# Attention's value products traced one half of the queries later, with the edge key blocks at 128 queries

## The chip, the cores and the metric

The kernel runs on one core of a Trainium2 chip. Its time is what the device takes for one execution of the whole program, in microseconds (us). The engines are named as the profile names them: PE is TensorE (with PEld, its weight loader), DVE is VectorE, ACT is ScalarE, POOL is GpSimd, SP is SyncE, whose queue starts most of the loads.

## What is computed

One layer of a hybrid encoder over 2048 tokens of width 1024, all in float32: a norm, one projection, banded attention beside an RWKV-7 recurrence, a gated merge, and a feed-forward part. The change touches the attention alone:

```python
# 8 heads of 64; a chunk is 64 tokens; a query sees its own chunk and the 8 before
scores = einsum('bnqhd,bnkhd->bnhqk', qc, kb) * 64 ** -0.5
scores = where(valid, scores + bias, -1e30)     # learned bias on clipped distance
p = softmax(scores, axis=-1)
out = einsum('bnhqk,bnkhd->bnqhd', p, vb)       # the value products
```

## The kernel before

**Float32 in two parts.** TensorE multiplies numbers rounded to its own float32r type. To keep float32 accuracy, an operand is split into a high part (ScalarE's rounding copy) and a low part (VectorE: source less high part), and a product is made of several matmuls. `split` (L65 to L67) does it for dense operands, `mm3` (L69 to L77) multiplies high by high, high by low and low by high.

**Stages.** The tokens go in four groups of 512. For each group there is a stage of the recurrence, then `phase_attention` (L915), then `phase_merge`. The feed-forward part follows after all four.

**Attention.** A group's 8 heads are four pairs (`att_pair`, L787). A pair first has its queries, keys and values projected (`dense`, L106; 24 matmuls of 512 columns each). The pools hold two pairs' `QA`, `QB`, `KK` and `VV`, so a pair can be projected while the one before it is in its softmax. Then, for each head of the pair (`par`) and each half of the group's queries (`half`, 256 queries), two blocks (`b`) of 128 queries go through:

1. scores against 640 keys into a PSUM tile that has one buffer (L851);
2. bias added and minimum taken by VectorE (L857), exponential by ScalarE (L862), scaling by VectorE (L865);
3. five transposes of 128 by 128 by TensorE (L869), again with one buffer;
4. the high part of the transposed probabilities, `PTh`, by ScalarE (L873), and the low part, `PTl`, by VectorE (L874).

A half's 256 queries see six key blocks of 128 (`kt` 0 to 5): the first block of queries sees 0 to 4, the second 1 to 5. So `PTh` and `PTl` are tiles of 128 x 6 x 256 in which two corners hold zeros, written once a group (L932, L933). There are two such pairs of tiles, used in turn. The value products of a half (L875 to L886) are twelve matmuls of 256 columns into one PSUM tile: the six key blocks with `PTh`, then the six with `PTl`. The stationary operand holds the values' high and low parts side by side, so the result's lower 64 rows and upper 64 rows are added afterwards: a copy (L883) and an addition into `ya` (L884). In the first group there are no keys before the group, so a half has two key blocks (4 and 5) or four (2 to 5). After a pair's four halves `ya` is split (L887) for the projection that follows.

**Other work at hand.** The second branch's projection (`branches`, L954, with the weights of `proj_b`) is traced at the end of `phase_attention`; its inputs come from the recurrence and don't wait for the attention.

**What sets the order.** The program is traced in Python and ordered by a planner when it is built. The planner follows each engine with estimated durations and gives it, among the instructions whose inputs and buffers it believes ready, the one that was traced first. Semaphores then keep the data right on the chip; an engine takes its instructions in the planned order and waits where an input is late. The order of tracing is thus an order of precedence, not the order of execution: with the tracing of before, a half's value products stand ahead of the next half's scores, and all of a pair's work ahead of the next pair's projections.

Of the kernel before, what the change touches and what calls it, by code (L numbers as in the profile page):

```python
# [2 lines left out]

# [5 lines left out]
F32 = mybir.dt.float32  # L9
# [3 lines left out]
ALU = mybir.AluOpType  # L13
# [36 lines left out]
class Block:  # L50
# [736 lines left out]
    def att_pair(self, g, p):  # L787
        nc, ap = self.nc, self.ap
        rows = [slice(0, C), slice(C, P)]
        first, lastg = g == 0, g == self.NG - 1  # L790
        KK = ap.tile([P, 2, 2, G], F32R, tag="KK", name="KK")
        VV = ap.tile([P, 2, GT, 2, 2, C], F32R, tag="VV", name="VV")
        if not first:
            kr = ap.tile([P, 2, G], F32, tag="kr", bufs=1, name="kr")
            nc.sync.dma_start(kr, self.kc[p])
            nc.scalar.copy(KK[:, :, 0], kr)
            vr = ap.tile([P, GT, 2, 2, C], F32, tag="kr", bufs=1, name="vr")
            nc.sync.dma_start(vr, self.vc[p])
            nc.scalar.copy(VV[:, 0], vr)

        ps = self.dense(ATT0 + p * P)
        QA = ap.tile([P, 2, G], F32R, tag="QA", name="QA")
        QB = ap.tile([P, 2, G], F32R, tag="QB", name="QB")
        for par in range(2):
            rw, ow = rows[par], rows[1 - par]
            nc.scalar.activation(QA[rw, par], ps[rw], AF.Copy, scale=-0.125)
            nc.scalar.activation(QB[ow, par], ps[rw], AF.Copy, scale=-0.125)
            for dst in (QB[rw, par], QA[ow, par]):
                nc.vector.scalar_tensor_tensor(
                    dst, ps[rw], -0.125, QA[rw, par].bitcast(F32), op0=ALU.mult, op1=ALU.subtract  # L810
                )
        ps = self.dense(ATT0 + HW + p * P)
        for par in range(2):
            rw, ow = rows[par], rows[1 - par]
            nc.scalar.copy(KK[rw, par, 1], ps[rw])
            nc.vector.tensor_tensor(KK[ow, par, 1], ps[rw], KK[rw, par, 1].bitcast(F32), ALU.subtract)
        ps = self.dense(ATT0 + 2 * HW + p * P)
        vf = ap.tile([P, G], F32, tag="vf", bufs=1, name="vf")
        nc.scalar.copy(vf, ps)
        pst = self.pt.tile([P, GT, P], F32, tag="t", name="ps_vt")  # L820
        for t in range(GT):
            nc.tensor.transpose(pst[:, t], vf[:, t * P : (t + 1) * P], self.ident)
        pv4 = pst.rearrange("p t (e d) -> p t e d", d=C)
        for t in range(GT):
            nc.scalar.copy(VV[:, 1, t, :, 0], pv4[:, t])
            nc.vector.tensor_tensor(VV[:, 1, t, :, 1], pv4[:, t], VV[:, 1, t, :, 0].bitcast(F32), ALU.subtract)
        if not lastg:
            nc.gpsimd.dma_start(self.kc[p], KK[:, :, 1].bitcast(F32))
            nc.gpsimd.dma_start(self.vc[p], VV[:, 1].bitcast(F32))

        ya = ap.tile([P, G], F32, tag="ya", name="ya")
        for par in range(2):
            bias = self.load_bias(2 * p + par)
            Kv = KK[:, par].rearrange("p h n -> p (h n)")
            for half in range(2):
                PTh, PTl = self.pts[self.npt % 2]
                self.npt += 1
                for b in range(2):
                    qb = half * 2 + b
                    k0 = qb * P if not first else G  # L840
                    n = (qb + 5) * P - k0
                    s0 = 640 - n
                    h1 = (n // 2) if n > 512 else n
                    pss = self.psc.tile([P, 1024], F32, tag="s", name="ps_s")
                    c0 = 512 - h1 if n > 512 else 0
                    qs = slice(qb * P, (qb + 1) * P)
                    for lo_, w in ((0, h1), (h1, n - h1)):
                        if not w:
                            continue
                        for i, q in enumerate((QA, QB)):  # L850
                            nc.tensor.matmul(  # L851
                                pss[:, c0 + lo_ : c0 + lo_ + w], q[:, par, qs],
                                Kv[:, k0 + lo_ : k0 + lo_ + w], start=i == 0, stop=i == 1,
                            )
                    sc = ap.tile([P, 640], F32, tag="sc", name="sc")
                    mn = ap.tile([P, 1], F32, tag="mn", bufs=4, name="mn")
                    nc.vector.tensor_tensor_reduce(  # L857
                        sc[:, 0:n], bias[:, s0:640], pss[:, c0 : c0 + n], 1.0, 3.0e38,
                        ALU.add, ALU.min, mn,
                    )  # L860
                    sm = ap.tile([P, 1], F32, tag="sm", bufs=4, name="sm")
                    nc.scalar.activation(sc[:, 0:n], sc[:, 0:n], AF.Exp, scale=-1.0, bias=mn, accum_out=sm)  # L862
                    rs = ap.tile([P, 1], F32, tag="rs", bufs=4, name="rs")
                    nc.vector.reciprocal(rs, sm)
                    nc.vector.tensor_scalar(sc[:, 0:n], sc[:, 0:n], rs, None, ALU.mult)  # L865
                    nk = n // P
                    pst = self.pt.tile([P, 5, P], F32, tag="t", name="ps_pt")
                    for j in range(nk):
                        nc.tensor.transpose(pst[:, j], sc[:, j * P : (j + 1) * P], self.ident)  # L869
                    kt0 = b + 5 - nk  # L870
                    hv = PTh[:, kt0 : kt0 + nk, b * P : (b + 1) * P]
                    lv = PTl[:, kt0 : kt0 + nk, b * P : (b + 1) * P]
                    nc.scalar.copy(hv, pst[:, 0:nk])  # L873
                    nc.vector.tensor_tensor(lv, pst[:, 0:nk], hv.bitcast(F32), ALU.subtract)  # L874
                pv = self.pv.tile([P, 2 * P], F32, tag="pv", name="ps_pv")  # L875
                kts = [kt for kt in range(6) if not first or half * 2 + kt >= GT]
                terms = [(x, kt) for x in (PTh, PTl) for kt in kts]
                for i, (x, kt) in enumerate(terms):
                    kb = half * 2 + kt
                    st = VV[:, kb // GT, kb % GT, par].rearrange("p s d -> p (s d)")  # L880
                    nc.tensor.matmul(pv, st, x[:, kt], start=i == 0, stop=i == len(terms) - 1)
                y2 = ap.tile([C, 2 * P], F32, tag="y2", name="y2")
                nc.scalar.copy(y2, pv[C:P])  # L883
                nc.vector.tensor_tensor(  # L884
                    ya[rows[par], half * 2 * P : (half + 1) * 2 * P], pv[0:C], y2, ALU.add
                )  # L886
        self.split(self.ya[0][:, p], self.ya[1][:, p], ya)  # L887

    def build_bias(self, sp, dp):

# [24 lines left out]
    def phase_attention(self, g):  # L915
        tc, nc = self.tc, self.nc
        self.yctx = ExitStack()
        yp = self.yctx.enter_context(tc.tile_pool(name="ya", bufs=1, side="right", reuse_waits="tile"))
        self.ya = self.alloc_y(yp)
        self.bp = self.yctx.enter_context(tc.tile_pool(name="br", bufs=2, side="right", reuse_waits="tile"))  # L920
        with ExitStack() as ctx:
            e = ctx.enter_context
            self.ap = e(tc.tile_pool(name="at", bufs=2, reuse_waits="tile"))
            pp = e(tc.tile_pool(name="atp", bufs=1, reuse_waits="tile"))
            self.psc = e(tc.tile_pool(name="atps", bufs=1, space=PSUM, reuse_waits="tile"))
            self.pt = e(tc.tile_pool(name="atpt", bufs=1, space=PSUM, reuse_waits="tile"))
            self.pv = e(tc.tile_pool(name="atpv", bufs=2, space=PSUM, reuse_waits="tile"))
            self.pts, self.npt = [], 0
            for i in range(2):
                t = [pp.tile([P, 6, 2 * P], F32R, name=f"PT{x}{i}") for x in "hl"]  # L930
                for y in t:
                    nc.gpsimd.memset(y[:, 0, P : 2 * P].bitcast(F32), 0.0)  # L932
                    nc.gpsimd.memset(y[:, 5, 0:P].bitcast(F32), 0.0)  # L933
                self.pts.append(t)
            for p in range(NP):
                self.att_pair(g, p)
            y = self.load_y(pp, self.ap)
            for i in range(KB // 2):
                nc.gpsimd.dma_start(self.md[i], self.branches(y, 1, i))
# [411 lines left out]
```

## Time and profile before

| | |
|---|---|
| median of 3 runs | 3420.65 us (3418.1 to 3421.2) |
| profiled execution | 3419.56 us, span of its instructions 3417.9 us |
| granted TensorE clock, mean | 0.988 |
| busy: PE, PEld, DVE, ACT, POOL | 96%, 78%, 71%, 41%, 12% |
| value products, L881 | 672 matmuls, in four stages between 340.3 and 1990.8 us |
| scores, L851 | 448 matmuls |
| transposes of probabilities, L869 | 560 |

A row of the profile gives line, engine, operation, the tiles written and read, the shape and the count, then busy time and the mean duration of one. In the timeline the first two columns are the start and the length in us, and brackets hold the idle time of that engine just before, with what ended it. A matmul's bar includes the time that its results take to come out, so bars overlap and the distance between starts tells more than a bar's length. A weight load (PEld) comes ahead of each matmul and may run while the matmul before it is still busy.

### The profile page before, as it was taken

Reading aid. Unit: us, or ns where it says so; the run is one execution under the profiler, and the core shown is the slowest. Engines: PE = TensorE matmul, PEld = TensorE weight load, DVE = VectorE, ACT = ScalarE, POOL = GpSimd, SP = SyncE. Lnnn points to the kernel's source line nnn. Section 1 sums busy time; section 2 is a strip of 40 time slices with the busy share of each in tenths; the row PEclk is TensorE's granted clock in tenths of the full one; section 3 lists DMA queues with packets and bytes.
Section 4 is the critical chain, followed back from the end, with each engine's and each line's share of the span. In section 5 each row is a group of like instructions: output and inputs, shape, how many; then the busy total and the mean of one; then the engine's idle time right before and its main releaser. Section 6 shows DMA issues by size and latency. Waiting matters only on the chain. (4 is left out here: it accounts for less than half of the span.)

```text
span 3417.9 us, 50375 instructions
## 1 busy us (share of the span) xinstructions
PE 3297.4 (96%) x19233; PEld 2675.8 (78%) x19233; DVE 2413.0 (71%) x4110; ACT 1414.0 (41%) x2319; POOL 419.8 (12%) x796
## 2 busy tenths in 40 slices
PE   7999999999999999999999989999999999999998
PEld 5777777777877777877777878888888878888886
DVE  5774856766866665875775875877887788676667
ACT  4434634436644445644445634333321243331112
POOL 2110002111022110021210000111200011100001
PEclk9999999999999999999999999999999999999999
DMA  5224353125373225374224276434845364343333
GB/s 147 84 81 129 131 188 120 56 88 188 122 276 115 62 93 168 124 270 127 74 92 140 91 271 215 136 114 156 290 161 178 105 234 136 114 145 99 99 99 111
DMA packets 397864, 481.10 MB, mean 141 GB/s; under 512 B 17516, under 2 KB 304432, under 8 KB 397624
## 3 DMA queue, kind: packets, MB, share of 16 engines
q1 hardware_dynamic: 346168, 364.63, 33.6%
q0 software_dynamic: 23040, 79.71, 6.1%
q10 hardware_dynamic: 28416, 33.56, 2.9%
q8 instruction: 151, 2.47, 0.3%
q14 instruction: 89, 0.73, 0.1%
HBM read 356.16 MB, written 124.81 MB: 141 GB/s over the span
## 5 line engine op out<-in xcount | busy, mean ns | idle before, releaser
L75 PE MATMUL ps_dn<-fop 128*128 128x512 f32 x3072 | 700.8, 390 | 2.0 <-DVE u L1229 2.0
L75 PEld LDWEIGHTS ps_dn<-fop 128*128 128x128 f32 x3072 | 575.6, 188 | 123.5 <-DVE u L1229 3.5
L75 PE MATMUL psd<-hh,whi 128*128 128x512 f32 x1344 | 543.2, 404 | 7.5 <-ACT whi L66 6.6
L75 PE MATMUL psd<-hl,whi 128*128 128x512 f32 x1344 | 542.5, 404 | 0.0
L75 PE MATMUL psd<-hh,wlo 128*128 128x512 f32 x1344 | 538.9, 401 | 0.6 <-DVE wlo L67 0.5
L66 ACT CAST whi<-wraw 128x1024 fp32r<-128x1024 f32 x232 | 243.3, 1049 | 511.0 <-PE psd L75 410.2
L1229 DVE TENSOR_TENSOR u<-u,ps_dn 128x512 f32<-128x512 f32 x480 | 323.2, 686 | 149.2 <-PE ps_dn L75 148.3
L67 DVE TENSOR_TENSOR wlo<-wraw,whi 128x1024 fp32r<-128x1024 f32 x232 | 282.9, 1220 | 203.0 <-ACT whi L66 185.1
L75 PEld LDWEIGHTS psd<-hh,whi 128*128 128x128 f32 x1344 | 257.4, 192 | 60.6 <-ACT whi L66 7.4
L75 PEld LDWEIGHTS psd<-hh,wlo 128*128 128x128 f32 x1344 | 257.1, 191 | 50.4 <-DVE wlo L67 2.0
L75 PEld LDWEIGHTS psd<-hl,whi 128*128 128x128 f32 x1344 | 257.2, 191 | 50.1
L66 ACT CAST fop<-wdraw 128x1024 fp32r<-128x1024 f32 x64 | 67.0, 1047 | 422.5 <-DVE u L1229 303.3
L1150 POOL DMA_DIRECT2D ad<-r x128 | 69.2, 541 | 586.8 <-DVE r L1149 557.2
L75 PE MATMUL ps_p<-yh,whi 128*128 128x512 f32 x256 | 103.5, 404 | 11.2 <-DVE th L964 8.5
L66 ACT CAST s12h<-s 128x1024 fp32r<-128x1024 f32 x32 | 33.8, 1055 | 184.6 <-PE ps_u L75 184.6
L992 PE MATMUL ps_o<-whi,mh 128*128 128x512 f32 x256 | 102.1, 405 | 7.9 <-ACT o L998 6.0
L857 DVE CUSTOM_DVE_ANT_0 sc<-bias,ps_s 128x640 f32<-128x640 f32 (+4 forms) x128 | 93.5, 730 | 22.2 <-PE ps_pt L869 18.1
L992 PE MATMUL ps_o<-wlo,mh 128*128 128x512 f32 x256 | 103.8, 405 | 3.7 <-DVE wlo L67 3.5
L862 ACT ACTIVATE sc<-sc,mn 128x640 f32<-128x640 f32 (+4 forms) x128 | 97.7, 764 | 19.3 <-DVE mn L857 18.7
L75 PE MATMUL ps_p<-yh,wlo 128*128 128x512 f32 x256 | 104.3, 407 | 0.5 <-DVE wlo L67 0.5
L873 ACT CAST PTh<-ps_pt 128x640 fp32r<-128x640 f32 (+4 forms) x128 | 79.9, 624 | 58.8 <-PE ps_pt L869 56.9
L75 PE MATMUL ps_p<-yl,whi 128*128 128x512 f32 x256 | 103.5, 404 | 0.0
(352 smaller groups left out, 6649.4 us busy)
## 6 DMA issues: line engine op xcount, KB each, us to landing
wraw<-in_w_in_dram SPq DMA_DIRECT2D x168, 512.0 KB
wraw<-in_w_up_dram SPq DMA_DIRECT2D x80, 512.0 KB
ad<-r POOLq DMA_DIRECT2D x128, 256.0 KB, 2.4
wdraw<-in_w_down_dram SPq DMA_DIRECT2D x64, 512.0 KB
araw<-ad SPq DMA_DIRECT2D x64, 512.0 KB
gd<-gate ACTq DMA_DIRECT2D x64, 256.0 KB
th<-gd SPq DMA_DIRECT2D x32, 512.0 KB
wraw<-in_w_out_dram SPq DMA_DIRECT2D x32, 512.0 KB
```

Source lines behind the costliest of these rows:

```text
L66: self.nc.scalar.copy(hi, src)
L67: self.nc.vector.tensor_tensor(lo, src, hi.bitcast(F32), ALU.subtract)
L75: mm = nc.tensor.matmul(ps, l, r, start=n == 0, stop=n == last).ins
L857: nc.vector.tensor_tensor_reduce(sc[:, 0:n], bias[:, s0:640], pss[:, c0 : c0 + n], 1.0, 3.0e38, ALU.add, ALU.min, mn,)
L862: nc.scalar.activation(sc[:, 0:n], sc[:, 0:n], AF.Exp, scale=-1.0, bias=mn, accum_out=sm)
L873: nc.scalar.copy(hv, pst[:, 0:nk])
L992: nc.tensor.matmul(ps[t], l[:, k, ts], r[:, k % 2], start=k == 0 and j == 0, stop=k == KB - 1 and j == 2)
L1150: nc.gpsimd.dma_start(self.ad[fb][:, th], r)
L1229: nc.vector.tensor_tensor(u[t][:, ns], u[t][:, ns], ps, ALU.add)
```

## The change

The value products move into a function of their own, `att_values`. `att_pair` calls it for the half before (held in `self.values`) at the place where it made the products of the present half, that is after the present half's transposes and casts are traced; the last half's are made after the last pair. So a half's value products, their copy and addition, and with a pair's last half the split of `ya`, come after the next half's scores and transposes in the order of tracing, and for the last half of a pair also after the next pair's projections.

Key blocks 0 and 5, the edges, are multiplied with the 128 queries that see them and not with all 256. The matmuls start with the key blocks that all 256 queries see, since the first one into the PSUM tile must cover it. The zeros in the corners are no longer read, nor written.

```diff
@@ att_pair, after a half's transposes and casts
-                pv = self.pv.tile([P, 2 * P], F32, tag="pv", name="ps_pv")
-                kts = [kt for kt in range(6) if not first or half * 2 + kt >= GT]
-                terms = [(x, kt) for x in (PTh, PTl) for kt in kts]
-                for i, (x, kt) in enumerate(terms):
-                    kb = half * 2 + kt
-                    st = VV[:, kb // GT, kb % GT, par].rearrange("p s d -> p (s d)")
-                    nc.tensor.matmul(pv, st, x[:, kt], start=i == 0, stop=i == len(terms) - 1)
-                y2 = ap.tile([C, 2 * P], F32, tag="y2", name="y2")
-                nc.scalar.copy(y2, pv[C:P])
-                nc.vector.tensor_tensor(
-                    ya[rows[par], half * 2 * P : (half + 1) * 2 * P], pv[0:C], y2, ALU.add
-                )
-        self.split(self.ya[0][:, p], self.ya[1][:, p], ya)
+                self.values()
+                self.values = functools.partial(self.att_values, p, VV, ya, first, par, half, PTh, PTl)
+
+    def att_values(self, p, VV, ya, first, par, half, PTh, PTl):
+
+        nc = self.nc
+        pv = self.pv.tile([P, 2 * P], F32, tag="pv", name="ps_pv")
+        kts = [kt for kt in range(6) if not first or half * 2 + kt >= GT]
+
+        edge = {0: slice(0, P), 5: slice(P, 2 * P)}
+        full = [kt for kt in kts if kt not in edge]
+        terms = [(PTh, kt) for kt in full]
+        terms += [(x, kt) for x in (PTh, PTl) for kt in kts if kt in edge]
+        terms += [(PTl, kt) for kt in full]
+        for i, (x, kt) in enumerate(terms):
+            kb = half * 2 + kt
+            st = VV[:, kb // GT, kb % GT, par].rearrange("p s d -> p (s d)")
+            qs = edge.get(kt, slice(0, 2 * P))
+            nc.tensor.matmul(pv[:, qs], st, x[:, kt, qs], start=i == 0, stop=i == len(terms) - 1)
+        y2 = self.ap.tile([C, 2 * P], F32, tag="y2", name="y2")
+        nc.scalar.copy(y2, pv[C:P])
+        qs = slice(half * 2 * P, (half + 1) * 2 * P)
+        nc.vector.tensor_tensor(ya[par * C : par * C + C, qs], pv[0:C], y2, ALU.add)
+        if par and half:
+            self.split(self.ya[0][:, p], self.ya[1][:, p], ya)
@@ phase_attention
                 t = [pp.tile([P, 6, 2 * P], F32R, name=f"PT{x}{i}") for x in "hl"]
-                for y in t:
-                    nc.gpsimd.memset(y[:, 0, P : 2 * P].bitcast(F32), 0.0)
-                    nc.gpsimd.memset(y[:, 5, 0:P].bitcast(F32), 0.0)
                 self.pts.append(t)
+            self.values = lambda: None
             for p in range(NP):
                 self.att_pair(g, p)
+            self.values()
```

More of the change, by code (lines that the diff above doesn't have):

```diff
@@ L1 @@
+import functools
 import math
```

## The prediction

> **What bounds the kernel now.** I read the page first, then the busy time of the four attention stages, then what TensorE's weight loads of the value products (line 881) wait for, and last the timeline around two of those waits.
>
> ```profile
> span 3417.9 us, 50375 instructions
> PE 3297.4 (96%) x19233; PEld 2675.8 (78%) x19233; DVE 2413.0 (71%) x4110; ACT 1414.0 (41%) x2319; POOL 419.8 (12%) x796
> ...
> core 0: us, PE busy (x) PEld busy (x) DVE busy (x) ACT busy (x) POOL busy (x), PEclk, DMA share, GB/s
> 330.00:436.00 106.00, 103.08 (x541) 80.64 (x540) 85.10 (x232) 69.08 (x167) 7.65 (x22) 1.00 0.42 141
> 805.00:949.00 144.00, 141.72 (x816) 116.77 (x816) 117.86 (x240) 95.68 (x181) 8.95 (x27) 1.00 0.44 147
> 1327.00:1472.00 145.00, 142.00 (x815) 116.71 (x815) 118.00 (x240) 95.67 (x180) 8.86 (x27) 1.00 0.42 144
> 1847.00:1991.00 144.00, 141.66 (x814) 116.63 (x815) 117.70 (x239) 95.47 (x179) 3.95 (x19) 1.00 0.35 116
> ```
>
> TensorE bounds the whole kernel (96%) and each of the four attention stages as well: in the second one it is busy 141.7 of 144 us, VectorE 117.9 (82%), ScalarE 95.7 (66%), the DMA engines 44%. The granted clock is 1.00 in all four, so none of this is throttling. Time that TensorE loses in these stages is therefore time of the kernel; time that VectorE, ScalarE or GpSimd saves there is not. But a matmul's bar includes its pipeline's tail, so a busy TensorE may still stand waiting for a weight load. That shows in the loads' own idle time:
>
> ```profile
> L881 PEld LDWEIGHTS ps_pv<-PTh,VV x336: 186/188/193, 340.3 to 1989.3; 128*128 128x128 f32 x168
> ...
> L881 PE MATMUL ps_pv<-PTl,VV x336: 274/281/387, 341.1 to 1990.8; 128*128 128x256 f32 x168
> ...
>   ACT PTh L873: 33.8, 104
>   DVE PTl L874: 3.3, 15
> ...
> PEld ps_pv L881 <- ACT PTh L873: 4.1, 16, 0.5
> PEld ps_pv L881 <- ACT PTh L873: 8.9, 25, 0.6
> PEld ps_pv L881 <- ACT PTh L873: 9.2, 26, 0.6
> PEld ps_pv L881 <- ACT PTh L873: 9.3, 26, 0.6
> ```
>
> The weight loader stood idle 33.8 us, in 104 places, until ScalarE had cast the transposed probabilities (line 873), and only 3.3 us until VectorE had their low part (line 874). The last four rows split it by stage: 4.1, 8.9, 9.2, 9.3 us. With 64 halves (16 per stage) that is more than one wait per half. The timeline shows which two; this is one of each kind:
>
> ```profile
> start us, us, engine line op out<-in xcount [idle before <-releaser]
> 858.40 0.69 ACT L873 CAST PTh<-ps_pt 128x640 fp32r<-128x640 f32 x1 [0.76 <-PE ps_pt L869]
> ...
> 858.83 0.40 PE L75 MATMUL psd<-hh,whi 128*128 128x512 f32 x1
> 859.14 0.66 PEld L881 LDWEIGHTS ps_pv<-PTh,VV 128*128 128x128 f32 x5 [0.35 <-ACT PTh L873]
> 859.14 0.87 PE L881 MATMUL ps_pv<-PTh,VV 128*128 128x256 f32 x5
> ...
> 859.85 0.28 PE L881 MATMUL ps_pv<-PTl,VV 128*128 128x256 f32 x1
> ...
> 860.55 0.76 PE L881 MATMUL ps_pv<-PTl,VV 128*128 128x256 f32 x5
> ...
> 862.16 0.39 PE L75 MATMUL psd<-hh,whi 128*128 128x512 f32 x1
> 862.39 0.39 PE L75 MATMUL psd<-hl,whi 128*128 128x512 f32 x1
> 862.79 0.19 PEld L881 LDWEIGHTS ps_pv<-PTh,VV 128*128 128x128 f32 x1 [0.45 <-ACT PTh L873]
> 862.80 0.39 PE L881 MATMUL ps_pv<-PTh,VV 128*128 128x256 f32 x1
> 863.02 0.31 PE L851 MATMUL ps_s<-KK,QA 128*128 128x320 f32 x1
> ```
>
> The first kind is the block of five behind the cast of a half's second query block. The second is a single product, that of key block 0: its second 128 queries are the zeros, so it is ready at the cast of the first query block, and the planner inserts it there, alone, a few matmuls too early. Matmuls of 512 columns start 0.23 us apart (862.16, 862.39), value products of 256 columns 0.12 us apart: (0.76 - 0.28) / 4. So the single product could have started at 862.62 and left TensorE at 862.74, but the next matmul starts at 863.02: 0.28 us lost, of 0.45 idle at the loader. At the block, 858.83 + 0.23 = 859.06 was possible, and counting back five products from 859.85 it effectively began at 859.25: 0.19 us lost, of 0.35. A wait thus costs TensorE its idle time less about 0.165 us.
>
> ```profile
> 820.99 0.19 PEld L881 LDWEIGHTS ps_pv<-PTh,VV 128*128 128x128 f32 x1 [0.36 <-issue]
> 831.05 0.66 PEld L881 LDWEIGHTS ps_pv<-PTh,VV 128*128 128x128 f32 x5 [0.29 <-ACT PTh L873]
> ...
> 943.91 0.19 PEld L881 LDWEIGHTS ps_pv<-PTh,VV 128*128 128x128 f32 x1 [0.35 <-ACT PTh L873]
> 946.62 0.65 PEld L881 LDWEIGHTS ps_pv<-PTh,VV 128*128 128x128 f32 x5 [0.34 <-ACT PTh L873]
> ```
>
> In the second stage the timeline has 16 single loads (first 820.99, last 943.91), 14 behind an idle stretch, 6.05 us together, and 16 blocks, 13 behind one (first of these 831.05, last 946.62), 3.87 us. The first stage has no singles, since key block 0 lies before the sequence there: its 16 waits are all of blocks.
>
> **The change part by part.** *The lone products go.* The new order begins each half with key blocks that meet all 256 queries, so nothing can start before the second query block's cast. 14 lone waits of 0.43 us (6.05 / 14) cost 0.27 us of TensorE each, 3.75 us a stage. The third and fourth stages have the same waits within 4% (9.2 and 9.3 against 8.9), so three stages give 11.3 us. Bounds: nothing, if the lost time turns up at the next crossing of engines, and 14.5 us, if a lone wait is worth 0.30. I take 11.3, the sum from rows. What follows sooner is the next matmul in the queue, mostly projections of the next pair, which have their weights; that is why I expect the gain to stay.
>
> *The value products are traced a half later.* Count and operands are the same: 672 products, 64 copies, 64 additions. The planner gives an engine, among the instructions that it believes ready, the one traced first. After the change the scores and transposes of the next half, but not the projections of the next pair, go ahead of a half's value products. Since the projections come later still, a block can be taken at the same moment as before: when the planner believes the cast done. Its estimate is too early by the same 0.3 us. So the trace order by itself need not remove the block's wait. Only the last half of each pair, 16 of 64, is put behind a whole pair's projections. The blocks' waits cost 3.87 - 13 x 0.165 = 1.7 us in each of three stages and 4.1 - 16 x 0.165 = 1.5 us in the first, 6.7 us in all. A quarter of it is 1.7 us: that is what I take, between nothing and 6.7.
>
> *Edge blocks at 128 columns.* Half the queries for key blocks 0 and 5, high and low: 4 products in each of 48 halves and 2 in each of the first stage's 16, so 224 of 672. What a product of 128 columns with its own weight load takes is seen at the first stage's scores:
>
> ```profile
> 329.89 0.39 PE L75 MATMUL psd<-hh,wlo 128*128 128x512 f32 x1
> ...
> 330.12 0.22 PE L851 MATMUL ps_s<-KK,QA 128*128 128x128 f32 x1
> 330.18 0.28 PE L851 MATMUL ps_s<-KK,QB 128*128 128x128 f32 x1
> ...
> 330.29 0.45 PE L75 MATMUL psd<-hh,whi 128*128 128x512 f32 x1
> ...
> 330.57 0.39 PE L75 MATMUL psd<-hl,whi 128*128 128x512 f32 x1
> ```
>
> The starts are 0.06 apart, but the bars grow (0.22, 0.28, 0.45), so the recorded starts run ahead. From 330.12 to 330.57 lie two of them and one of 512 columns: 0.45 - 0.23 = 0.22, or 0.11 each. Against 0.12 that saves 0.01 us, 2.2 us in all. Ends: nothing (half the columns and the same weight load), and 0.12 - 0.06 = 0.06 each, 13.4 us, if the starts were true. I take 2.2, since the second 512-column matmul only comes when the first three are through.
>
> The Trainium skill ("TensorE: Matmul & The Clock Gate", "LDWEIGHTS") puts a load of 128 weight columns at 128 / 1.2 GHz = 107 ns whatever moves behind it. That speaks against the halved columns as a saving, and the trace's 0.11 agrees. The same page ("Back-to-back issue gap") gives 81 ns for a sustained pair of load and 128-column matmul. By that the edges would save 224 x 0.039 = 8.7 us, an estimate, and the total be near 3398; but its companion figure of 131 ns at 512 columns isn't this trace's 0.23 us, so I leave it at a small chance.
>
> *Zeros not written.* 32 fills by GpSimd leave:
>
> ```profile
> L932 POOL MEMSET PTh<- x8: 223/224/226, 319.6 to 1842.9; 128x128 f32 x8
> L933 POOL MEMSET PTl<- x8: 222/224/225, 320.0 to 1843.4; 128x128 f32 x8
> ```
>
> That is 32 x 0.224 = 7.2 us of an engine at 12%, at each stage's start, while TensorE runs projections; the cover is over 10 us long (319.6 to the first scores at 330.1). Worth nothing. Were that cover gone, 1.8 us a stage.
>
> *What is moved along.* A half's copy of the upper rows, its addition and, once a pair, the split of `ya` (a cast and a subtraction) come a half later. No DMA moves: the loads on SP's queue and the stores on GpSimd's stay in their order. `VV` of a pair is held a quarter of a pair's time longer, until the first half of the next pair is through; its slot is wanted by the pair after that, whose values are projected in the three halves left. Nothing waits, by my reading; were a value projection held up, other projections stand ready for TensorE. The probability buffers (two sets) are tighter: the cast two halves later overwrites the set that the postponed products read. That is a rival below.
>
> **The sum.** 3419.56 (the profiled execution; its span is 3417.9, and 1.1 us under the median of the runs) - 11.3 - 1.7 - 2.2 = 3404.4, or 3405.5 beside the median. I say 3405.
>
> **Rivals.** *Everything goes.* The planner, with scores and transposes to choose first, hides the blocks' waits too: another 5 us (6.7 less the 1.7 taken), 3399. With edges at their recorded starts, another 11.2 (13.4 less 2.2), about 3388. For it: a waiting block is next to ready products only where something else is traced ahead. Against it: the projections are still traced behind.
>
> *The wait only moves.* TensorE comes 0.27 us earlier to the next score or transpose and waits there for VectorE or ScalarE. Then only the edges are left: 3419.56 - 2.2 = 3417.4, no change. For it: VectorE is at 82% and its softmax steps are a chain. Against it: TensorE's queue holds projections between almost all of those steps.
>
> *Slower: the probability sets.* If the products of a half stay behind until the transposes of the half after next, the cast (line 873) must wait for them; ScalarE is in order, and behind it stand the exponentials of the next block. From the cast at 858.40 to the next one at 862.05 (its products were quoted at 862.79) there are 3.65 us for a block of twelve, 1.43 us. It decides where over 2 us of other work is taken in between. With 0.5 us lost in each of 64 halves it is 32 us, less the 15.2 above: 3436.
>
> ```profile
> 862.05 0.69 ACT L873 CAST PTh<-ps_pt 128x640 fp32r<-128x640 f32 x1
> ```
>
> **How the numbers follow.** The forecast (3396 to 3412) has 45%, everything 18%, the wait that moves 24%, slower 13%. A difference under 0.2% (6.8 us) is about what a measurement of this kernel cannot tell from none. So faster is 63%, same 24%, slower 13%. The range of 8 in 10 takes in the edges' full saving and ends just past the moved wait: 3388 to 3424. The first two cases alone lie between 3388 and 3412.
>
> **What would show it.** No single load of line 873's high part any more in front of a value product; the loader's idle time for that cast down from 33.8 us in 104 places to about 15 in 50 to 60; value products of two widths, 224 and 448, the narrow ones 0.11 us apart; the attention stages from the second on shorter by 4 to 5 us, the first by under 1. The edges' step is wrong if narrow products stand 0.06 apart in a run of four. The placing is wrong if the blocks' waits vanish as well, and the forecast if the time lost before line 881 comes back before scores or transposes, or if the casts wait for value products.

## The result and the profile after

The changed kernel takes 3443.75 us (3439.4 to 3444.8, four runs) against 3420.93 of the kernel before: 1.0070 times as long, 95% interval 1.0057 to 1.0082. The forecast was 3405, with a range up to 3424. The profiled execution took 3439.39 us. All times are medians; runs that took some 6% or more longer than the others of their kernel are left out of them (two runs of `n2_bias_early`, one each of `e6_e4_order_narrow`, `f1_two_transpose_buffers`, `h1_first_pairs_later` and `h2_last_pair_later`). From here on a line of the kernel after is one higher up to the casts (L870 transposes, L874 and L875 casts), and the value products are L894.

The page's head and the attention stages' windows of the changed kernel, laid where the stages now are; columns as before (length, then PE, PEld, DVE, ACT, POOL busy, granted clock):

```profile
span 3437.7 us, 50303 instructions
PE 3300.4 (96%) x19233; PEld 2679.5 (78%) x19233; DVE 2410.8 (70%) x4110; ACT 1417.7 (41%) x2319; POOL 410.3 (12%) x764
...
330.00:436.00 106.00, 101.34 (x527) 78.40 (x526) 84.88 (x232) 68.67 (x167) 7.98 (x22) 1.00 0.40 132
812.00:956.00 144.00, 138.25 (x801) 114.71 (x800) 114.18 (x237) 94.43 (x177) 8.04 (x24) 1.00 0.42 140
1336.00:1481.00 145.00, 140.40 (x810) 116.35 (x809) 115.62 (x239) 96.13 (x180) 8.08 (x25) 1.00 0.42 140
1862.00:2006.00 144.00, 138.47 (x797) 115.45 (x796) 114.69 (x238) 95.58 (x179) 3.42 (x18) 0.99 0.34 109
```

TensorE has as many matmuls as before (19233), but in windows of equal length fewer fit: 527 for 541, 801 for 816, 810 for 815, 797 for 814. It is not throttled: the granted clock is 0.99 to 1.00 in these windows, as before. It stands still more.

What the value products wait for, in the view of their line:

```profile
L894 PE MATMUL ps_pv<-PTh,VV x336: 218/280/390, 340.9 to 2001.9; 128*128 128x256 f32 x120, 128*128 128x128 f32 x48
L894 PE MATMUL ps_pv<-PTl,VV x336: 220/281/367, 342.1 to 2003.2; 128*128 128x256 f32 x104, 128*128 128x128 f32 x64
...
  ACT PTh L874: 9.7, 35
  DVE PTl L875: 1.2, 4
who waited for it (us, times):
  ACT y L896: 10.1, 17
  PEld ps_pt L870: 5.8, 10
```

The edit does what it says, and more than was forecast at this line: the idle time for the high part, ahead of matmuls and of their weight loads together, falls from 33.8 us in 104 places to 9.7 in 35, that for the low part from 3.3 to 1.2. Of the forms listed, 48 of 168 and 64 of 168 have 128 columns, together one third: the 224 in 672 of the forecast. No cast (L874) is among those who waited for a value product, so the probability sets, the slow rival's mechanism, did not bind.

The time is elsewhere. From the list of waits of the weight loader over the whole span (us in total, times, longest), rows of the attention with others between them left out, the kernel before and then after:

```profile
PEld ps_pv L881 <- ACT PTh L873: 31.6, 93, 0.6
PEld ps_s L851 <- DVE mn L857: 8.4, 36, 0.7
PEld ps_vt L822 <- ACT vf L819: 6.5, 6, 2.0
PEld ps_pt L869 <- issue: 6.1, 19, 0.7
PEld ps_pt L869 <- DVE VV L826: 4.3, 6, 1.8
```

```profile
PEld ps_pt L870 <- issue: 13.0, 34, 0.9
PEld ps_vt L823 <- ACT vf L820: 12.1, 16, 3.0
PEld ps_pt L870 <- DVE PTl L875: 11.0, 36, 0.5
PEld ps_s L852 <- DVE mn L858: 10.0, 38, 0.5
PEld ps_pv L894 <- ACT PTh L874: 9.5, 34, 0.7
PEld ps_pt L870 <- PE ps_pv L894: 5.8, 10, 0.7
PEld ps_pt L870 <- DVE VV L827: 5.1, 8, 1.9
```

The transposes (`ps_pt`) and, through the PSUM buffer that they share, the values' transposes (`ps_vt`) took the waits over: in the rows of all groups the idle time ahead of the transposes' loads is 18.0 us before and 40.1 after:

```profile
L869 PEld LDWEIGHTS ps_pt<-ident,sc 128*128 128x128 f32 x560 | 65.3, 140 | 18.0 <-issue 6.1 <-DVE VV L826 4.3 <-DVE PTl L874 1.1
L870 PEld LDWEIGHTS ps_pt<-ident,sc 128*128 128x128 f32 x560 | 61.3, 140 | 40.1 <-issue 13.0 <-DVE PTl L875 11.0 <-PE ps_pv L894 5.8
```

How close TensorE now runs to VectorE is seen at the scaling (L865, now L866), the last step ahead of a block's transposes. Its line's waiters, the kernel before and after:

```profile
  PE ps_pt L869: 0.2, 1
```

```profile
  PE ps_pt L870: 5.0, 18
```

And in the timeline, scalings and transposes alone, before and after:

```profile
851.06 0.56 DVE L865 TENSOR_SCALAR sc<-sc,rs 128x640 f32<-128x640 f32 x1
852.48 0.55 DVE L865 TENSOR_SCALAR sc<-sc,rs 128x640 f32<-128x640 f32 x1
853.91 0.77 PE L869 MATMUL ps_pt<-ident,sc 128*128 128x128 f32 x5
857.60 0.71 PE L869 MATMUL ps_pt<-ident,sc 128*128 128x128 f32 x5
```

```profile
840.90 0.55 DVE L866 TENSOR_SCALAR sc<-sc,rs 128x640 f32<-128x640 f32 x1
841.59 0.74 PE L870 MATMUL ps_pt<-ident,sc 128*128 128x128 f32 x5
844.83 0.55 DVE L866 TENSOR_SCALAR sc<-sc,rs 128x640 f32<-128x640 f32 x1
845.53 0.74 PE L870 MATMUL ps_pt<-ident,sc 128*128 128x128 f32 x5 [0.30 <-DVE sc L866]
848.66 0.54 DVE L866 TENSOR_SCALAR sc<-sc,rs 128x640 f32<-128x640 f32 x1
849.36 0.74 PE L870 MATMUL ps_pt<-ident,sc 128*128 128x128 f32 x5
```

Before, two scaled blocks lie ready and transposes come 2.3 us (853.91 - 851.62) and 4.6 us (857.60 - 853.03) behind their scaling. After, they come 0.14, 0.15 and 0.16 us behind it: TensorE takes these blocks the moment they are there, and has none in hand when one is late. Of the 96 blocks of stages two to four 33 are taken within 0.2 us of their scaling, where it was 3 before.

**Where TensorE stands.** For a sum over the stages I took from each trace the start of every matmul to the next, less the spacing of its kind while TensorE is fed (0.227 us for 512 columns, 0.174 for 384, 0.145 for 320, 0.119 for 256, 0.110 for 128 and for transposes). Part I runs from a stage's start to the first branch product or the last projection, whichever is first; II from there to the last value product; III to the first product of the merge; IV to its last. "Slack" is the mean time from a scaling's end to its transposes, over the 96 blocks of stages two to four. Times are medians, the other columns are of the profiled execution, all in us; the profiled execution of `e4_terms_only` took 3425.2 us, the longest of its ten runs, that of `h1_first_pairs_later` 3427.2, the shortest of its four.

| kernel | time | I | II | III | IV | sum | slack |
|---|---|---|---|---|---|---|---|
| before | 3420.9 | 38.2 | 8.1 | 23.1 | 22.0 | 91.5 | 2.21 |
| after | 3443.8 | 49.5 | 11.6 | 26.9 | 28.2 | 116.2 | 1.08 |
| `e4_terms_only` | 3417.5 | 37.1 | 7.0 | 26.4 | 27.6 | 98.0 | 2.20 |
| `e6_e4_order_narrow` | 3415.8 | 37.2 | 7.3 | 18.3 | 32.6 | 95.4 | 2.16 |
| `e9_only_pair_end` | 3419.8 | 35.1 | 8.5 | 21.8 | 30.5 | 95.9 | 2.11 |
| `h2_last_pair_later` | 3424.2 | 38.7 | 5.5 | 28.2 | 23.6 | 95.9 | 2.16 |
| `d1_after_scores` | 3426.6 | 38.8 | 8.9 | 26.5 | 27.2 | 101.3 | 2.04 |
| `e8_flush_pair` | 3428.0 | 42.2 | 8.5 | 26.0 | 27.5 | 104.2 | 1.72 |
| `h1_first_pairs_later` | 3433.4 | 45.6 | 8.2 | 19.1 | 32.3 | 105.2 | 1.70 |
| `e5_narrow_zeros_kept` | 3440.7 | 48.7 | 9.1 | 29.6 | 28.1 | 115.5 | 1.83 |
| `e1_order_only` | 3441.8 | 46.3 | 9.2 | 24.7 | 33.4 | 113.6 | 1.87 |

Of the 24.7 us that TensorE stands longer (the two profiled executions are 19.8 us apart, so some 5 us come back outside these parts), 11.3 are in part I, 3.5 in II, and 10 in III and IV, where the branch products and the merge stand. III and IV differ by as much between kernels that are of like times, so they carry the loss less clearly. Part I is what tells the kernels apart: 35 to 39 us in those near the time of before, 45 to 50 in those 12 us and more above it. It does not give the time by itself: the four kernels whose profiled execution took 3427 to 3429 us (`h2`, `d1`, `e8`, `h1`) have 38.7, 38.8, 42.2 and 45.6. By what the wait stood in front of, in part I:

| kernel | value products | transposes | `ps_vt` | scores | projections |
|---|---|---|---|---|---|
| before | 15.1 | 5.9 | 5.1 | 5.1 | 7.0 |
| after | 4.9 | 20.1 | 10.3 | 8.2 | 6.0 |
| `e1_order_only` | 9.2 | 8.0 | 8.9 | 8.8 | 11.4 |
| `e5_narrow_zeros_kept` | 22.8 | 9.4 | 5.9 | 5.9 | 4.8 |
| `e4_terms_only` | 13.0 | 4.8 | 6.6 | 4.8 | 7.8 |

The predicted gain is in the first column (10.2 us); 22.5 us came back in the next three.

### The profile page after: what moved, and what is told of

Same layout as the page of the kernel before. It is cut to its first block, busy times and chain, and to the rows that moved or that the text cites. A ratio compares the mean times of both kernels' runs of the same rounds, so it can differ in the third digit from the quotient of the medians.

```text
span 3437.7 us, 50303 instructions
## 1 busy us (share of the span) xinstructions
PE 3300.4 (96%) x19233; PEld 2679.5 (78%) x19233; DVE 2410.8 (70%) x4110; ACT 1417.7 (41%) x2319; POOL 410.3 (12%) x764
## 5 line engine op out<-in xcount | busy, mean ns | idle before, releaser
L76 PE MATMUL ps_p<-yh,whi 128*128 128x512 f32 x256 | 105.3, 411 | 14.5 <-DVE th L976 14.5
L874 ACT CAST PTh<-ps_pt 128x640 fp32r<-128x640 f32 (+4 forms) x128 | 79.9, 624 | 66.3 <-PE ps_pt L870 63.7
L875 DVE TENSOR_TENSOR PTl<-ps_pt,PTh 128x640 fp32r<-128x640 f32 (+4 forms) x128 | 94.4, 738 | 16.6 <-ACT PTh L874 15.6
L1004 PE MATMUL ps_o<-whi,ml 128*128 128x512 f32 x256 | 104.1, 407 | 0.0
```

What stands on the lines that cost most here:

```text
L76: mm = nc.tensor.matmul(ps, l, r, start=n == 0, stop=n == last).ins
L1004: nc.tensor.matmul(ps[t], l[:, k, ts], r[:, k % 2], start=k == 0 and j == 0, stop=k == KB - 1 and j == 2)
```

## The experiments

**Each part alone.** The order alone (products traced a half later, 256 columns, key block 0 first, zeros kept), the edges alone (old place), and the whole change with the products traced one block of 128 queries later in place of a half. The edits here and below are shortened:

```diff
 e1_order_only: as after, but
-        edge = {0: slice(0, P), 5: slice(P, 2 * P)}
+        edge = {}
+        terms = [(x, kt) for x in (PTh, PTl) for kt in kts]
 e2_edges_only: as after, but
-                self.values()
-                self.values = functools.partial(self.att_values, p, VV, ya, first, par, half, PTh, PTl)
+                self.att_values(p, VV, ya, first, par, half, PTh, PTl)
 e3_quarter_later: as after, but, inside the loop over b
-                self.values()
+                    if b == 0:
+                        self.values()
+                        self.values = lambda: None
```

> The value products are traced one half later as in the changed kernel, but all are 256 queries wide, key block 0 first, and the corners hold zeros. Theory A (precedence): the later place gives the next half's scores and transposes precedence over the products, and the time saved before the products comes back before the transposes and at the stage's end; then this alone is slow, about 3440 us, with the transposes' excess over 15 us. Theory B (edges): the narrow products or their order cost the time; then this is at or under 3421 us. Theory C (scatter): any other order of tracing moves the plan by some 20 us without a rule; then this lies anywhere from 3400 to 3445.

> The value products stay where they were traced before; only the edge blocks are 128 queries wide, the full blocks come first and the zeros go. Theory A: the lone products go and nothing pays for it, 3405 to 3412 us. Theory B: 3435 to 3445 us. Theory C: anywhere from 3400 to 3445.

> Everything as in the changed kernel, but a half's value products are traced after the first of the next half's two query blocks, so half as late. Theory A: between edges alone and the changed kernel, about 3425 us. Theory B: as the changed kernel, 3440 us. Theory C: anywhere from 3400 to 3445.

Measured: the order alone 3441.8 us (ratio 1.0045 to 1.0075), the edges alone 3437.2 (1.0034 to 1.0064), the third 3444.4 (1.0054 to 1.0088). Each part by itself costs most of the loss (21 and 17 us), and they do not add: both make 23 us, not 38. One block later is as bad as two, where theory A had it half as bad. Theory A's time for the order alone came (about 3440), its row did not: the transposes stand 2.1 us longer in part I, not 15.

**Which part of the edges, and is it scatter?** The term order alone (full blocks first, 256 columns, old place); narrow edges with the zeros still written; and two edits of before that change the trace without touching the value products.

```diff
 e4_terms_only: as e2, with the zeros, and
-            qs = edge.get(kt, slice(0, 2 * P))
+            qs = slice(0, 2 * P)
 e5_narrow_zeros_kept: as e2, with the zeros
 n1_swap_two: as before, but
-            for dst in (QB[rw, par], QA[ow, par]):
+            for dst in (QA[ow, par], QB[rw, par]):
 n2_bias_early: as before, but
+        biases = [self.load_bias(2 * p + par) for par in range(2)]
-            bias = self.load_bias(2 * p + par)
+            bias = biases[par]
```

> Traced as before, 256 queries wide and with zeros; only the order of the twelve products is that of the changed kernel (the four full key blocks first). It tells the lone product's removal from the narrow width. Theory A: the lone product's 11 us are gained here too, 3407 to 3414 us, and the difference to edges alone is the width's 2 us. Theory B: if the order of terms is what costs, 3435 to 3445 us. Theory C: anywhere from 3400 to 3445.

> Edges alone again (traced in the old place, 128 queries for the edge blocks, full blocks first), but the zeros are still written by GpSimd, and read by nothing. It parts the width from the fills. If the narrow width is what costs edges alone its 17 us, this stays at 3435 to 3440 us. If the missing fills cost it, by what they change in the plan, this returns to 3415 to 3421 us. Theory C (scatter) gives neither, only a value within 3400 to 3445.

> The kernel before with one pair of equal VectorE instructions traced in the other order (the two low parts of the queries). No work changes. Theories A and B, in which the edits themselves cost: within 3 us of the kernel before. Theory C (any change of tracing moves the plan by some 20 us): 3430 us or more, or 3410 or less.

> The kernel before with both heads' bias loads traced at the pair's start and not the second one after the first head. Same instructions; none of them is waited for in the trace. Theories A and B: within 3 us of the kernel before. Theory C: 3430 us or more, or 3410 or less.

Measured: term order 3417.5 us (0.9981 to 1.0000), narrow with zeros 3440.7 (1.0046 to 1.0076), swapped 3421.0 (0.9994 to 1.0013), bias early 3421.0 (0.9993 to 1.0013). Term order missed theory A's 3407 to 3414. The zeros are worth nothing, and it is the edit to 128 columns that costs, at the old place some 23 us. The last two kernels say little of scatter: in their traces the planned order is all but that of before (`n2_bias_early` has the same sequence on TensorE, VectorE and ScalarE, `n1_swap_two` differs in the swapped pairs on VectorE). More is said by `e4_terms_only` here and `e9_only_pair_end` below, whose sequences on TensorE differ from before at about 1000 and 1800 of 19233 places, and the slow `e5_narrow_zeros_kept` at about 1800: a new order as such need not cost 20 us. That these slow orders are slow by a rule, and would be so in another kernel, is not shown by that.

**Is it the columns, or the order that the planner makes of them?** Two kernels whose matmuls get their width after the planner has ordered everything:

```diff
 e6_e4_order_narrow: as e4; e7_e5_order_wide: as e5, the other way round
         Block(tc, aps, out[0]).run()
+    edges(nc)     # cut key blocks 0 and 5 to 128 columns (e7: widen them) in the finished program
```

> The planner orders everything with products of 256 columns (the order of the kernel with new terms only, 3417.5 us); after it has ordered them, the 224 edge products are cut to their 128 columns. So the order on every engine is that of the wide kernel, and only what TensorE executes is narrow. Theory P (it is the planner's other order that costs 17 to 23 us when the edges are narrow, the products themselves save about 5 ns each): 3414 to 3418 us. Theory W (a narrow product itself costs the time, by its weight load or by what stands behind it): 3434 to 3441 us.

> The converse: the planner orders everything with the edges at 128 columns (the order of the kernel with narrow edges and the zeros kept, 3440.7 us); after it has ordered them, the edge products are widened to 256 columns, over the zeros. Theory P: the loss stays with the order, 3440 to 3443 us. Theory W: the loss goes with the columns, 3418 to 3424 us.

Measured: 3415.8 us (0.9974 to 0.9992) and 3437.7 (1.0036 to 1.0064), the second 2 us under theory P's range but far from W's. Theory P. With the wide kernel's order the narrow products take 3415.8 for 3417.5; with the narrow kernel's order the wide ones take 3437.7 for 3440.7. The columns themselves are worth nothing that these runs resolve; the order costs 20 to 25 us. What the value products (L893 here) and their weight loads waited for, in the four kernels (wide order `e4`, `e6`; narrow order `e5`, `e7`):

```profile
  ACT PTh L874: 19.8, 60
  DVE PTl L875: 2.5, 13
```

```profile
  ACT PTh L874: 19.3, 60
  DVE PTl L875: 2.7, 13
```

```profile
  ACT PTh L874: 21.3, 65
  DVE PTl L875: 17.6, 47
```

```profile
  ACT PTh L874: 24.6, 66
  DVE PTl L875: 16.6, 45
```

The rows go with the order and not with the columns. In the narrow order the wait for VectorE's subtraction comes 45 to 47 times, not 13, which is 14 to 15 us more of idle time, 10.5 to 11 of them at the loader. The sequence on TensorE shows why. The second product with the low part is the first that needs the second query block's subtraction. In the narrow order all twelve products stand in a row in 36 of the 48 halves that have twelve, in the wide order in 3; in the other 45 one to six other matmuls stand behind the first product with the low part, and cover the subtraction. By starts TensorE stands 12.3 us between products with the low part in `e5`, 9.9 in `e7`, 1.7 in `e4` and `e6`: of the 13.7 us by which `e5` exceeds `e4` in parts I and II, 10.6 are here. In the changed kernel this wait is gone again (1.2 us, 4 times), as the products come a half later, which fits that the two losses do not add.

**How much later, and where.** One dose less than the change (values traced right behind the next half's first scores), and four kernels with the order alone that limit where it acts:

```diff
 d1_after_scores: as e1, but self.values() stands behind the first block's scores
 e8_flush_pair: as e1, and at a pair's end
+        self.values()
+        self.values = lambda: None
 e9_only_pair_end: as e1, and after each half
+                if not (par and half):
+                    self.values(); self.values = lambda: None
 h1_first_pairs_later: the same with
+                if p == NP - 1 or (p == NP - 2 and par and half):
 h2_last_pair_later: the same with
+                if p < NP - 1:
```

> Order only, with a smaller step: full width, zeros kept, key block 0 first, and a half's value products traced right after the next half's first scores, so that four score matmuls and nothing else of the next half go ahead of them. Theory A (the transposes' precedence costs): near the kernel before, 3415 to 3424 us. If any precedence of the next half costs as much: 3438 to 3445 us. Theory C: anywhere from 3400 to 3445.

> Order alone (256 columns, zeros, key block 0 first, as in the kernel with the order alone, 3441.8 us), but the last half of each pair has its products traced at the pair's end, as in the kernel before; the other three halves of a pair stay one half later. Theory B (the loss comes from the pair's boundary, where the last half now stands behind a whole pair's projections): 3419 to 3425 us. Theory I (it comes from inside the pairs, where scores and transposes go ahead of the products and use up the time over which projections were spread): 3436 to 3442 us. Half and half would be 3429 to 3433.

> Order alone, and only for the last half of each pair: its products are traced after the first half of the next pair; the other three halves are traced at their old place. Theory B: 3436 to 3442 us. Theory I: 3419 to 3425 us. Half and half would be 3429 to 3433.

> The order alone (256 columns, zeros, key block 0 first), one half later in a stage's first three pairs only; in the fourth pair, beside which the branch products run, every half's products are traced at their old place, and those of the third pair's last half at that pair's end. Theory Q (the loss is that branch products lose their place beside the last pair's softmax): 3417 to 3426 us. Theory I (it is made inside the pairs, evenly): 3433 to 3440 us.

> The converse: the first three pairs of a stage at their old place, only the fourth pair's value products one half later. Theory Q: 3434 to 3442 us. Theory I (a quarter of the pairs, a quarter of the loss): 3423 to 3428 us.

Measured: 3426.6 us (1.0005 to 1.0025), 3428.0 (1.0013 to 1.0030), 3419.8 (0.9987 to 1.0005), 3433.4 (1.0024 to 1.0052), 3424.2 (0.9994 to 1.0015). Going past the next half's first scores costs 6 us; past that block's transposes and casts as well, 24 (`e3`, which has the edges, too); past the whole half, 21. A pair's end alone costs nothing, so theory B falls. With all halves but a pair's last it is 7, so theory I did not hold in full either. In the first three pairs it costs 13 us, in the last pair at most 5 by its interval: these two lie in theory I's ranges and outside those of Q, the theory of the next question. By the medians neither division adds up to the 21.

**Do the branch products lose their place?** Branch products on TensorE inside the time from a stage's start to its last value product, second stage, in windows of that tile alone (length, PE, PEld, DVE): before, after, `h1`, `h2`.

```profile
792.90:948.60 155.70, 21.67 (x77) 13.46 (x77) 4.11 (x6) 1.00 0.45 150
```

```profile
797.50:951.10 153.60, 14.55 (x51) 8.90 (x52) 2.73 (x4) 1.00 0.42 141
```

```profile
791.80:947.00 155.20, 19.19 (x66) 11.63 (x66) 3.41 (x5) 1.00 0.45 150
```

```profile
795.20:950.90 155.70, 21.48 (x77) 13.40 (x77) 4.08 (x6) 1.00 0.45 150
```

After, 51 fit in for 77, in about the same time. `h2`, in which the last pair's products are the late ones, keeps all 77. Is that the loss, or a sign of it? Two kernels keep them all out, with the old order and with the later one:

```diff
 g1_branches_after: as before; g2_order_branches_after: as e1
+            with tc.issue_after(self.last.ins):      # self.last: the last value product
                 for i in range(KB // 2):
                     nc.gpsimd.dma_start(self.md[i], self.branches(y, 1, i))
```

> The kernel before, with TensorE's branch products (line 75, ps_p) all queued behind a stage's last value product. In the kernel before 67 to 77 of a stage's 192 stand beside the last pair's softmax, 16 to 18 us of TensorE a stage; without them that softmax has no cover. Estimate: 3455 to 3490 us. It serves as the base of the next kernel.

> The kernel with the order alone (3441.8 us, 21 above the kernel before), with the branch products queued behind the last value product in the same way. Theory Q (the later order loses its time because fewer branch products fit beside the last pair's softmax, 51 to 56 instead of 67 to 77, and the rest stands alone at the stage's end): at most 9 us above the kernel before with the same edit, or under it. Theory I (the loss is made inside the pairs, whatever stands at the stage's end): 17 to 24 us above it, as without the edit.

Measured: 3498.5 us (3495.9 to 3507.9) and 3490.1 (3486.7 to 3501.9), so the later order is 8 us the faster here by the medians, with runs that overlap; the first is above its range, the second where Q had it, under the kernel that it is compared with. But the sums over the traces say otherwise: in part I the later order stands 47.8 us for 38.9, 9 more, and with branch products it was 8 more (46.3 for 38.2); in part II it stands 63.1 for 76.2. It loses in the first three pairs as ever, and gains in the last one, where now nothing but value products can cover a softmax. What the value products' first loads waited for, `g1` and then `g2`, has that gain:

```profile
L881 PEld LDWEIGHTS ps_pv<-PTh,VV 128*128 128x128 f32 x336 | 50.7, 201 | 57.7 <-ACT PTh L873 54.4 <-issue 2.4 <-POOL bias L912 0.7
```

```profile
L891 PEld LDWEIGHTS ps_pv<-PTh,VV 128*128 128x128 f32 x336 | 50.6, 201 | 39.5 <-ACT PTh L874 35.9 <-issue 2.7
```

The kernels limited to three pairs and to one say the same. The later order helps an uncovered softmax; in the kernel as it is, the branch products and projections are that cover already. That is a reading of the sums and of `h1` and `h2`; by its time alone this pair of kernels fits Q. (`g2`'s profiled execution took 3501.9 us, at the upper end of its runs; its parts I and II are shorter than `g1`'s by 4.2 us all the same.)

**Is it the transposes' one buffer?** A second slot in PSUM for `ps_pt`, and its control with the same packing and one slot:

```diff
+            self.tt, self.ntt = self.pt.tile([P, 12, P], F32, name="ps_t2"), 0
+            self.pv2, self.npv = self.pv.tile([P, 2, 2 * P], F32, name="ps_pv"), 0
+    def slot(self, n):
+        self.ntt += 1
+        k = 6 * (self.ntt % 2)        # c1_one_transpose_buffer: k = 0
+        return self.tt[:, k : k + n]
```

> The changed kernel with a second buffer in PSUM for the transposes (line 870 writes ps_pt, one buffer before; to make room the two buffers of the value products share a bank). In the changed kernel the weight loads of the transposes stand idle 11.0 us for line 875, the subtraction that reads the buffer last. Theory T (the later order pushes transposes closer together, and they wait for the one buffer; about 17 us of the loss are there): 3424 to 3432 us. Rival (the buffer is only where the lost time shows; it moves on to the next wait): 3440 to 3448 us.

> The control for the kernel with two transposes' buffers: the same edit, the value products' buffers in one bank and the transposes' tile kept for the whole stage, but every transpose in its first buffer. Both theories: as the changed kernel, 3440 to 3448 us. If it is faster than that, the packing and not the second buffer did it.

Measured: 3441.9 us (1.0039 to 1.0067) and 3443.9 (1.0045 to 1.0071). It tells nothing of the buffer. The rows of the transposes' loads are the same in both, `f1` and then `c1`:

```profile
L870 PEld LDWEIGHTS ps_t<-ident,sc 128*128 128x128 f32 x560 | 62.1, 141 | 37.4 <-DVE sc L866 16.0 <-DVE PTl L875 12.3 <-DVE VV L827 6.5
```

```profile
L870 PEld LDWEIGHTS ps_t<-ident,sc 128*128 128x128 f32 x560 | 61.8, 140 | 37.4 <-DVE sc L866 15.9 <-DVE PTl L875 12.3 <-DVE VV L827 6.5
```

The instructions stand in the same order on every engine (but for two pairs of matmuls in the recurrence), and in neither trace does a block's first transpose start before the subtraction of the block before has ended. The second slot was there and was not used ahead of time. Both slots lie in one tile; a tile for each was not tried, so whether theory T is right stays open. The rows do add one thing: with this packing the largest part of the wait is for the scaling itself (16 us), which a second buffer would not take away.

## Why the prediction was wrong

*The lone products go: right at its row, wrong in its worth.* `e4_terms_only` makes this step alone, at the old place. The idle time for the cast falls from 33.8 us in 104 places to 19.8 in 60. All 48 lone products are gone; the waits of the blocks behind them grew by about 3 us. By starts TensorE stands only 2.1 us less ahead of the value products in part I (13.0 for 15.1), with 1.5 more at `ps_vt` and 0.8 more at the projections: 37.1 us for 38.2 in all. The time is 2.7 us lower by the medians, with an interval that reaches no change. The step that failed is the sentence that "what follows sooner is the next matmul in the queue, mostly projections", from which the 11.3 us were kept. The rival in which the wait only moves had 24%, and its size (3417.4) is what this kernel shows (3417.5); its place is not, since neither scores (4.8 for 5.1) nor transposes (4.8 for 5.9) took the wait over.

*The value products a half later.* I priced the order at a gain of 1.7 us, with nothing as the worse end: the bound below nothing was missing. The reasoning was that projections, traced later still, would be taken as before. What I did not ask is what the instructions that now go ahead would wait for. Scores and transposes need VectorE's and ScalarE's last step, and value products were the work that kept TensorE busy until then. The order alone costs 21 us. Part I shows it at all neighbours: scores, `ps_vt` and projections 3.7 to 4.4 us each, transposes 2.1, less 5.9 at the value products. The sentence "the time lost before line 881 comes back before scores or transposes" named the sign; it came back there, in the changed kernel with 22.5 us for the 10.2 saved.

*The blocks' waits.* Forecast to stay in three of four. Of 58 of them, 16.7 us, the changed kernel has 35, 9.7 us, left. More went than forecast, and it did not help.

*Edges at 128 columns.* The price of a product was close: 2.2 us of gain forecast, nothing resolved (a gain of 1.7 us in one order, a loss of 3.0 in the other). In the changed kernel two narrow products in a row start 0.107 us apart, near the forecast 0.11 and far from 0.06. What was missing is that the planner orders by its own durations, and that a new duration makes a new order: 20 to 25 us. I had costed an edit of operands as if everything around it stayed.

*Zeros, and what moves along.* Worth nothing, as forecast: 3440.7 with, 3437.2 without, intervals that overlap. The slow rival came near the time (3436) for a reason that was not at work.

*Three readings.* The 33.8 us in 104 places were called the weight loader's; they are the loader's 31.6 in 93 and the matmuls' 2.2 in 11, and the four rows by stage are the loader's alone. The bound of 14.5 us goes with all 48 lone products at 0.30 (14.4), not with the 14 waits a stage that had been counted (12.6). The 0.11 us set beside the weight load is a distance of starts; the load's own rows read 0.186 to 0.193 us, so the agreement is one of the spacing and not of the load's length. The forecast hangs on none of them.

**What is shown and what is argued.** Shown by runs: the order alone, and the planner's order of the narrow edges alone, each make most of the loss; the columns do not; the loss of the order alone lies mostly in the first three pairs of a stage, where the projections run. That the smaller slack is why (1.70 to 1.87 us and less in the kernels 7 us and more above before, 2.0 to 2.2 in those within 6) fits the rows of the scaling and of the transposes, but slack was not changed by itself, and among the former it does not rank the times: the changed kernel has 1.08 us and the order alone 1.87, at times 2 us apart. Nor are blocks taken more often within 0.2 us of their scaling in the order alone (3 of 96, as before). So for the order alone the mechanism stays open beyond its rows: more idle time ahead of scores, `ps_vt` and projections. For the narrow edges at the old place it is read from the trace (the products in a row, and the subtraction), not tested by itself. Open are also the 10 us in parts III and IV.

The fastest kernel here is `e6_e4_order_narrow`: 3415.8 us, 0.9983 of before (0.9974 to 0.9992). It has the new term order and the narrow products in the wide order, without the later tracing; `e4_terms_only` is as fast within the measurement.

## What to carry to other kernels

Work that is ready late in a chain, here the value products, can be the cover for the steps of the chain that follow it; before giving other work precedence over it, ask what that other work waits for, and count that wait as a cost from zero upwards. Idle time at one loader's row is not yet time of the kernel: see whether the next instruction on that engine has its inputs. Where a planner orders the program, an edit of a size is an edit of the order, and the two can be told apart by changing the size after the ordering.

## What the runs showed of the hardware

Halving the columns of 224 of 672 products, each with its own weight load, made the kernel 1.7 us faster in one order (3415.8 for 3417.5) and 3.0 us slower in the other (3440.7 for 3437.7): no cost and no gain that these runs can tell. I had expected a gain of 2.2 us. By starts, two products of 128 columns in a row are 0.107 us apart in the changed kernel (median of 126 pairs), those of 256 columns 0.120.
